# Every second product of the adaptive parameters on POOL and ACT instead of DVE

## The chip, the cores and the metric

The kernel runs on one core of a Trainium2 chip. The metric is the device time of one execution in microseconds (us). The engines named below are PE (matrix products), PEld (its weight loads), DVE (vector), ACT (scalar), POOL (GpSimd) and SP (the queue that issues most DMAs).

## The reference

Two blocks follow each other on 256 tokens of width 1024. The first has two layers, each with a mixer (latent attention and a chunked mLSTM) and a convolutional FFN; the second is one layer with three token mixers and a hierarchical mixture of 32 experts. Each layer takes its shifts, scales and gates from a conditioning vector c, by one product of a vector with a 1024 x 6144 matrix. That product is what the change touches:

```python
c_act = jax.nn.silu(c)
for l in range(DEPTH):
    mod = (c_act @ ada_w[l] + ada_b[l])[:, None, :]
    sh1, sc1, g1, sh2, sc2, g2 = jnp.split(mod, 6, axis=-1)
    h = _rmsnorm(x, norm_mix_w[l]) * (1 + sc1) + sh1
    x = x + g1 * _mixer(h, ...)
    h = _rmsnorm(x, norm_ffn_w[l]) * (1 + sc2) + sh2
    x = x + g2 * _conv_ffn(h, ...)
```

The second block has the same form, and uses its matrix w_ada twice: all six parts for the tokens (c_2), and the first two parts for a context of 256 tokens (c_ctx_2).

## The kernel before

**Weights.** Nearly all matrix products are made of float32 split in two: a weight block of 128x1024 is loaded, ACT casts it to a rounded form (`hi`, line 451), DVE takes the residual (`lo`, line 453), and PE makes three products for each pair of operands (lines 474 to 476). `load` (line 442) brings 128x2048 at a time into a tile `raw` of which there are three; all such loads, weights and the matrix of the adaptive parameters alike, are issued on SP in program order, each when its tile is free. `hi` and `lo` have three tiles each.

**Adaptive parameters.** `ada` (line 524) makes the product with c. Its matrix is stored transposed, so an output lies on a partition: one load gives two blocks `w` of 128 outputs x 1024 inputs. For each block one DVE operation (line 533) multiplies it with c (a tile `cb`, the same on all partitions, which holds twice the SiLU of c), by 0.5, and sums along the row into one column of `mod`. The operation writes its product back into `raw`; the profile shows it with a short read of the accumulator after it. A part is a 1024-wide slice of the six: four loads, eight columns, and then one addition of the bias (line 536).

**Order.** `ada` is a generator: it yields after each load. In the context pass at the start its first two parts are made in the foreground, since the first projections need them (`context`, with four `raw` tiles of its own). The first two parts of layer 0 then run in the background of the context pass, and ADA_PARTS (line 36) spreads the other sixteen parts over mixer 0 (4 parts), FFN 0 (3), mixer 1 (5) and FFN 1 (4). `tick` steps the background generators at fixed rates at points in the program. Within an engine the order is fixed when the program is made; each engine works through its own in that order, and waits where an operand or a tile isn't ready.

**Stages in the trace.** Context pass to about 110 us, mixer 0 to 335, FFN 0 to 560, mixer 1 to 775, FFN 1 to 1015, the second block's mixers to about 1315, and the experts to the end. The FFN's only regular work on POOL is the residual of its hidden values (`split` at line 459, tile `hidl`). DVE's line 1033 adds a product in PSUM to `x`.

Of the kernel before, what the change touches and what calls it, by code (L numbers as in the profile page):

```python
# [15 lines left out]
AF = mybir.ActivationFunctionType  # L16
OP = mybir.AluOpType
# [334 lines left out]
class Net:  # L352
# [162 lines left out]
    def silu_row(self, c, eng=None):  # L515
# [5 lines left out]
        nc.vector.scalar_tensor_tensor(t, th, 1.0, t, OP.add, OP.mult)  # L521
        return t

    def ada(self, src, c, bias, mod, parts, pool=None):

        nc = self.nc
        for s in parts:
            for q in range(4 * s, 4 * s + 4):
                raw = self.load(src[q], pool, 3 if pool is None else CX_RAW)
                for r in range(2):  # L530
                    j = 2 * q + r
                    w = raw[:, r * 1024 : r * 1024 + 1024]
                    nc.vector.scalar_tensor_tensor(w, w, 0.5, c, OP.mult, OP.mult, accum_out=mod[:, j : j + 1])  # L533
                yield
            m = slice(8 * s, 8 * s + 8)
            nc.vector.tensor_tensor(mod[:, m], mod[:, m], bias[:, m], OP.add)
# [1632 lines left out]
```

## Time and profile before

| | |
|---|---|
| median of 3 runs | 1775.16 us (1772.66 to 1775.33) |
| the profiled execution | 1772.79 us, its span 1770.9 us |
| PE busy | 1579.1 us, 89% |
| DVE busy | 1128.0 us, 64% |
| ACT busy | 758.6 us, 43% |
| POOL busy | 77.9 us, 4% |
| mean granted clock of PE | 0.946 of full speed |

Busy times are sums over instructions of the one profiled execution; a busy PE is not PE at its peak, since its ends are modelled. The chain that ended last is followed back from the last instruction, at each step to what released it. An engine's idle time off that chain costs nothing.

### The profile page before, as it was taken

The numbers are of one execution on the slowest core, as the hardware profiler recorded it, in microseconds if no ns is written. First come the engines' busy times: TensorE is split into PE (matmuls) and PEld (weight loads), VectorE is DVE, ScalarE is ACT, GpSimd is POOL, SyncE is SP. The second block draws the span as 40 slices with busy tenths as digits, with TensorE's granted clock in tenths as the row PEclk, the third lists the DMA queues.
The fourth block names the chain that finished last, engine by engine and source line by source line (L and its number), as shares of the span: only waits on it lengthen the run. The fifth ranks groups of instructions, "written<-read, shape, count | busy, mean of one in ns | idle before, by whom it ended". The sixth has DMA issues, their size and how long they took to land.

```text
span 1770.9 us, 32054 instructions
## 1 busy us (share of the span) xinstructions
PE 1579.1 (89%) x13278; PEld 1269.7 (72%) x13278; DVE 1128.0 (64%) x2167; ACT 758.6 (43%) x1256; POOL 77.9 (4%) x81
## 2 busy tenths in 40 slices
PE   3989999999998999989999999999989877776766
PEld 2988999899998899979999999878874312221211
DVE  7979878798887898879989778766662111011011
ACT  3566545664455654556454576464431100000000
POOL 0000000020010000001010101000000000000000
PEclk7999999999999999999999999998989889888888
DMA  9745675556674478565667543123369999999998
GB/s 392 312 142 191 242 281 204 209 207 221 217 250 143 169 266 319 216 237 179 239 228 289 194 171 114 67 98 134 144 249 403 419 417 416 417 416 419 419 417 340
DMA packets 76808, 460.78 MB, mean 260 GB/s; under 512 B 8563, under 2 KB 11123, under 8 KB 28147
## 3 DMA queue, kind: packets, MB, share of 16 engines
q1 hardware_dynamic: 74352, 452.45, 67.0%
q10 hardware_dynamic: 2306, 6.24, 1.0%
q8 instruction: 106, 1.74, 0.4%
q14 instruction: 44, 0.35, 0.1%
HBM read 457.61 MB, written 1.05 MB: 259 GB/s over the span
## 4 chain that ended last, share of the span: by engine, by line
PE 63%; DMA 23%; DVE 8%; ACT 4%; issue 2%; POOL 0%; SPq 0%; DVEq 0%; ACTq 0%; POOLq 0%
DMA ew<-in_wgu 11%; PE d L474 10%; PE d L476 10%; PE d L475 10%; DMA ew<-in_wdown 8%; PE y L474 4%; PE y L476 3%; PE y L475 3%; PE a L1392 3%; DVE lo L453 2%; PE d L2052 2%; DVE raw L533 2%; PE a L1981 1%; PE a L628 1%; DMA raw<-in_ws 1%
## 5 line engine op out<-in xcount | busy, mean ns | idle before, releaser
L451 ACT CAST hi<-raw 128x1024 fp32r<-128x1024 f32 x309 | 322.4, 1048 | 303.2 <-PE d L475 186.2
L453 DVE TENSOR_TENSOR lo<-raw,hi 128x1024 fp32r<-128x1024 f32 x309 | 379.1, 1233 | 90.3 <-ACT hi L451 88.5
L474 PE MATMUL d<-hhi,hi 128*128 128x256 f32 x1320 | 387.9, 295 | 29.4 <-ACT hhi L591 23.7
L475 PE MATMUL d<-hlo,hi 128*128 128x256 f32 x1320 | 381.3, 289 | 3.2 <-DVE hlo L594 1.7
L476 PE MATMUL d<-hhi,lo 128*128 128x256 f32 x1320 | 380.2, 288 | 0.2 <-DVE lo L453 0.2
L474 PEld LDWEIGHTS d<-hhi,hi 128*128 128x128 f32 x1320 | 258.4, 196 | 38.3 <-ACT hhi L591 26.3
L475 PEld LDWEIGHTS d<-hlo,hi 128*128 128x128 f32 x1320 | 259.3, 196 | 6.6 <-DVE hlo L594 2.9
L476 PEld LDWEIGHTS d<-hhi,lo 128*128 128x128 f32 x1320 | 259.0, 196 | 1.4 <-DVE lo L453 0.4
L2052 PE MATMUL d<-ew,xe 128*32 128x512 f32 x984 | 165.3, 704 | 56.5 <-DMA ew<-in_wgu 56.0
L533 DVE SCALAR_TENSOR_TENSOR raw<-raw,cb 128x1024 f32<-128x1024 f32 x160 | 193.9, 1228 | 5.4 <-DMA raw<-in_ada 5.0
L2052 PEld LDWEIGHTS d<-ew,xe 128*32 128x32 f32 x984 | 26.1, 116 | 170.5 <-DMA ew<-in_wgu 145.7
L2057 DVE SCALAR_TENSOR_TENSOR moa<-moa,d 128x512 f32<-128x512 f32 x8 | 5.5, 687 | 178.4 <-ACT moa L2056 178.4
L474 PE MATMUL y<-hhi,hi 128*128 128x256 f32 x352 | 100.8, 286 | 4.6 <-ACT raw L685 3.9
L476 PE MATMUL y<-hhi,lo 128*128 128x256 f32 x352 | 100.0, 285 | 0.9 <-DVE lo L453 0.9
L475 PE MATMUL y<-hlo,hi 128*128 128x256 f32 x352 | 99.6, 283 | 0.0
L2070 PE MATMUL y<-ew,mht 128*32 128x512 f32 x472 | 74.4, 687 | 26.6 <-DMA ew<-in_wdown 22.4
L2088 DVE SCALAR_TENSOR_TENSOR x<-f,mod_l,x 128x256 f32<-128x256 f32 x32 | 14.0, 479 | 127.8 <-PE f L2084 127.8
L459 POOL TENSOR_TENSOR hidl<-fgel,hidh 128x256 fp32r<-128x256 f32 x44 | 54.2, 1233 | 838.4 <-ACT hidh L458 817.3
L2056 ACT ACTIVATE moa<-d 128x512 f32<-128x512 f32 x8 | 4.8, 597 | 184.7 <-PE d L2052 184.7
L474 PEld LDWEIGHTS y<-hhi,hi 128*128 128x128 f32 x352 | 67.4, 192 | 6.1 <-ACT raw L685 4.7
L2070 PEld LDWEIGHTS y<-ew,mht 128*32 128x32 f32 x472 | 13.0, 117 | 78.3 <-DMA ew<-in_wdown 58.6
L476 PEld LDWEIGHTS y<-hhi,lo 128*128 128x128 f32 x352 | 67.4, 192 | 1.4 <-DVE lo L453 1.1
(676 smaller groups left out, 3193.7 us busy)
## 6 DMA issues: line engine op xcount, KB each, us to landing
raw<-in_ws SPq DMA_DIRECT2D x151, 1024.0 KB, 4.8
ew<-in_wgu SPq DMA_DIRECT2D x100, 1024.0 KB, 18.0
raw<-in_ada SPq DMA_DIRECT2D x80, 1024.0 KB, 4.9
ew<-in_wdown SPq DMA_DIRECT2D x46, 1024.0 KB, 19.7
ew<-in_wgu SPq DMA_DIRECT2D x46, 512.0 KB, 13.8
ew<-in_wdown SPq DMA_DIRECT2D x28, 512.0 KB, 12.5
two<-in_wgu SPq DMA_DIRECT2D x20, 256.0 KB, 8.4
two<-in_wdown SPq DMA_DIRECT2D x16, 256.0 KB, 8.1
```

The lines of the kernel that those rows point to most:

```text
L451: f.append(nc.scalar.copy(hi_, raw))
L453: f.append(nc.vector.tensor_tensor(lo_, raw, hi_.bitcast(F32), OP.subtract))
L459: (eng or self.nc.vector).tensor_tensor(lo, src, hi.bitcast(F32), OP.subtract)
L474: nc.tensor.matmul(out, whi, hhi, start=first and i == 0, stop=False, **s)
L475: nc.tensor.matmul(out, whi, hlo, start=False, stop=False, **s)
L476: nc.tensor.matmul(out, wlo, hhi, start=False, stop=last and i == n - 1, **s)
L533: nc.vector.scalar_tensor_tensor(w, w, 0.5, c, OP.mult, OP.mult, accum_out=mod[:, j : j + 1])
L628: self.nc.tensor.transpose(out, in_, self.C("ident")[:k, :k])
L1392: nc.tensor.matmul(ps[r, g * 64 : g * 64 + 64], l_(g, p, r), r_(g, p, r), start=True, stop=True, skip_group_check=True)
L1981: nc.tensor.matmul(ps[:, k * P : k * P + P], xn[:, i, d : d + P], of(i), start=i == 0, stop=i == 1, skip_group_check=True)
L2052: nc.tensor.matmul(ps[32 * e : 32 * e + 32, :], xe[:, k, 32 * e : 32 * e + 32], w[e], start=k == 0, stop=k == 7, skip_group_check=True)
L2070: nc.tensor.matmul(py[q][32 * e : 32 * e + 32, :], ht[:, f * P + 32 * e : f * P + 32 * e + 32], w[e], start=f == 0, stop=f == 3, skip_grou ...
```

## The change

A new function makes the product of one block. For the first block of each load POOL multiplies the block with c in place, and ACT then copies the result in place with the factor 0.5 and sums along the row; the second block stays as it was, one DVE operation. Loads, tiles, parts, rates and the addition of the bias are unchanged.

```diff
--- before.py
+++ after.py
@@ -521,6 +521,15 @@
         nc.vector.scalar_tensor_tensor(t, th, 1.0, t, OP.add, OP.mult)
         return t
 
+    def ada_block(self, w, c, out, shared):
+
+        nc = self.nc
+        if shared:
+            nc.gpsimd.tensor_tensor(w, w, c, OP.mult)
+            nc.scalar.activation(w, w, AF.Copy, scale=0.5, accum_out=out)
+        else:
+            nc.vector.scalar_tensor_tensor(w, w, 0.5, c, OP.mult, OP.mult, accum_out=out)
+
     def ada(self, src, c, bias, mod, parts, pool=None):
 
         nc = self.nc
@@ -528,9 +537,7 @@
             for q in range(4 * s, 4 * s + 4):
                 raw = self.load(src[q], pool, 3 if pool is None else CX_RAW)
                 for r in range(2):
-                    j = 2 * q + r
-                    w = raw[:, r * 1024 : r * 1024 + 1024]
-                    nc.vector.scalar_tensor_tensor(w, w, 0.5, c, OP.mult, OP.mult, accum_out=mod[:, j : j + 1])
+                    self.ada_block(raw[:, r * 1024 : r * 1024 + 1024], c, mod[:, 2 * q + r : 2 * q + r + 1], r == 0)
                 yield
             m = slice(8 * s, 8 * s + 8)
             nc.vector.tensor_tensor(mod[:, m], mod[:, m], bias[:, m], OP.add)
```

## Rows read from the trace of the kernel before

**Rows 1.** Page, parts 1 and 4: busy time, and the chain by engine.

```profile
PE 1579.1 (89%) x13278; PEld 1269.7 (72%) x13278; DVE 1128.0 (64%) x2167; ACT 758.6 (43%) x1256; POOL 77.9 (4%) x81
...
PE 63%; DMA 23%; DVE 8%; ACT 4%; issue 2%; POOL 0%; SPq 0%; DVEq 0%; ACTq 0%; POOLq 0%
```

**Rows 2.** Table of stretches: length, then busy PE, PEld, DVE, ACT, POOL.

```profile
41.00:110.00 69.00, 67.15 (x521) 64.28 (x521) 61.52 (x111) 42.74 (x56) 0.72 (x2) 0.95 0.71 273
110.00:335.00 225.00, 210.42 (x1675) 200.70 (x1674) 179.71 (x316) 129.33 (x213) 0.00 (x0) 0.99 0.61 220
...
560.00:775.00 215.00, 200.04 (x1556) 190.23 (x1555) 178.10 (x316) 119.54 (x202) 0.49 (x2) 0.97 0.65 237
```

**Rows 3.** Chain's shares by line: 0:50, 110:300, 335:560, 560:775.

```profile
by line: DMA raw<-in_ws 26.0%; DMA x<-in_xT 24.1%; DMA raw<-in_ada 17.5%; DVE raw L533 13.9%; DVE lo L453 4.7%; ACT hhi L591 2.7%; ACT hi L451 2.1%; issue 1.8%; ACT two L561 1.5%; SPq L442 1.4%; DVE two L590 1.0%; SPq L519 0.8%; ACTq L382 0
by line: PE d L474 14.1%; PE d L475 13.5%; PE d L476 13.2%; DVE lo L453 7.7%; DVE raw L533 5.7%; issue 4.5%; DVE cacc L765 3.2%; ACT hi L451 2.7%; DMA raw<-in_ws 2.5%; PE a L628 2.2%; PE a L847 1.8%; PE a L884 1.4%; ACT L548 1.4%; ACT L549 
by line: PE d L474 14.8%; PE d L475 14.3%; PE d L476 14.0%; PE y L474 13.1%; PE y L476 12.8%; PE y L475 12.5%; PE a L1392 5.8%; DVE lo L453 2.3%; issue 1.8%; DVE two L590 1.1%; PE a L1370 1.1%; DVE x L1033 1.0%; PE a L1479 0.7%; PE a L628 0
by line: PE d L474 15.1%; PE d L475 15.0%; PE d L476 14.9%; DVE lo L453 5.9%; DVE raw L533 4.7%; issue 3.1%; PE a L628 2.1%; PE a L847 2.0%; PE d L487 1.9%; ACT hi L451 1.9%; PE d L488 1.8%; PE d L489 1.8%; DVE cacc L765 1.7%; PE a L898 1.6
```

**Rows 4.** Groups of DVE (to 1010 us) and ACT (to 1000), by form.

```profile
L453 DVE TENSOR_TENSOR lo<-raw,hi 128x1024 fp32r<-128x1024 f32 x268 | 328.5, 1232 | 84.0 <-ACT hi L451 82.3
L533 DVE SCALAR_TENSOR_TENSOR raw<-raw,cb 128x1024 f32<-128x1024 f32 x160 | 193.9, 1228 | 5.4 <-DMA raw<-in_ada 5.0
...
L855 ACT ACTIVATION_READ_ACCUMULATOR esm<-a,mx 128x1 f32 x32 | 6.3, 197 | 0.0
...
L520 ACT ACTIVATE cbt<-cb 128x1024 f32<-128x1024 f32 x3 | 3.2, 1057 | 3.3 <-DMA cb<-in_c_c 3.3
```

**Rows 5.** POOL's two-input operations by source line: minimum/median/maximum in ns.

```profile
L459 POOL TENSOR_TENSOR hidl<-fgel,hidh x44: 726/1298/1825, 360.5 to 1008.3; 128x256 fp32r<-128x256 f32 x44
...
L1728 POOL TENSOR_TENSOR two<-two,kon x8: 994/999/1108, 1183.3 to 1283.4; 128x384 f32<-128x384 f32 x8
```

**Rows 6.** Timeline, three places: start us, duration us, engine, line, operation.

```profile
364.51 2.90 DVE L453 TENSOR_TENSOR lo<-raw,hi 128x1024 fp32r<-128x1024 f32 x2
...
364.71 1.61 POOL L459 TENSOR_TENSOR hidl<-fgel,hidh 128x256 fp32r<-128x256 f32 x1 [2.68 <-ACT hidh L458]
...
401.69 0.73 POOL L459 TENSOR_TENSOR hidl<-fgel,hidh 128x256 fp32r<-128x256 f32 x1 [5.79 <-ACT hidh L458]
401.78 0.88 DVE L1033 SCALAR_TENSOR_TENSOR x<-d,mod,x 128x256 f32<-128x256 f32 x2
...
860.86 1.82 POOL L459 TENSOR_TENSOR hidl<-fgel,hidh 128x256 fp32r<-128x256 f32 x1 [8.63 <-ACT hidh L458]
860.86 1.22 DVE L453 TENSOR_TENSOR lo<-raw,hi 128x1024 fp32r<-128x1024 f32 x1
```

**Rows 7.** Timeline of the start.

```profile
16.27 1.22 DVE L533 SCALAR_TENSOR_TENSOR raw<-raw,cb 128x1024 f32<-128x1024 f32 x1 [3.20 <-DMA raw<-in_ada]
...
27.29 2.36 DVE L453 TENSOR_TENSOR lo<-raw,hi 128x1024 fp32r<-128x1024 f32 x2 [1.19 <-ACT hi L451]
...
34.27 0.17 DVE L536 TENSOR_TENSOR mod_c<-mod_c,vec 128x8 f32<-128x8 f32 x1
...
35.82 0.80 PE L474 MATMUL d<-hhi,hi 128*128 128x256 f32 x2 [14.79 <-ACT hhi L591]
```

**Rows 8.** Table of stretches for line 453 alone (DVE).

```profile
110.00:335.00 225.00, 73.02 (x60) 0.99 0.61 220
```

**Rows 9.** Waits: engine, line, waited for: us in total, times, longest.

```profile
ACT hi L451 <- PE d L475: 186.2, 118, 7.2
...
ACT hi L451 <- DMA raw<-in_ws: 35.7, 27, 5.3
...
SPq L442 <- DVE raw L533: 192.9, 59, 9.1
```

**Rows 10.** Groups of ACT: loads of activation tables, the largest group.

```profile
L541 ACT ACT_TABLE_LOAD x25 | 32.1, 1283 | 0.4
```

## Prediction

> **What bounds the kernel now.** I read the page first: PE is busy 89% of the span, DVE 64%, ACT 43%, POOL 4%; the chain that ended last runs 63% on PE, 23% on DMA, 8% on DVE and 4% on ACT [rows 1]. So the change takes work from an engine with a small share of the chain and gives it to the idlest one. Where on the chain that DVE share lies decides, so the second view is the table of stretches [rows 2]. The reader is to see that PE is busy 67 of 69 us in 41:110, but only 210 of 225 us in the first mixer (110:335) and 200 of 215 us in the second (560:775). The expert stage from about 1315 us on holds none of the changed products; what happens before it moves it as a whole. Third, the chain by line in four stretches [rows 3]: the products (line 533) make 13.9% of 0:50 (7 us), 5.7% of 110:300 (10.8 us) and 4.7% of 560:775 (10.1 us); in FFN 0 (335:560) they are not among the lines named.
>
> **What it removes.** There are 160 products of 128x1024, two for each of 80 loads; 193.9 us of DVE, 1.21 us each [rows 4]. The change takes the first of each load: 80 products, 97 us of DVE. 8 lie in the first context pass (before 35 us), 8 in the second (to 110 us), 16 in mixer 0, 12 in FFN 0, 20 in mixer 1, 16 in FFN 1 (parts 0 and 1 twice, then ADA_PARTS, 4 loads a part). Only what lies on the chain can come back. In the mixers that is at most half of 20.9 us: -10.5 us. In the FFNs and the second context pass PE covers it: 0.
>
> **What POOL pays.** No POOL product of 128x1024 is in the trace. The nearest rows are its two-input operations: 726 ns at best with 256 columns, 999 ns median with 384 [rows 5]. That is 2.13 ns a column, so 999 + 640 x 2.13 = 2.36 us; with no fixed part at all it would be 2.66 us (999 x 1024/384). I take 2.36 us.
>
> **What DVE pays for POOL.** The rows show POOL and DVE holding each other up. At 364.71 POOL starts a product beside two residuals (lo); they take 2.90 us together, where an undisturbed pair takes 2.36 us [rows 6, 7]: the second one was held for 0.54 us. At 860.86 both start at once, the residual keeps its 1.22 us and POOL's 256-column product takes 1.82 us instead of 0.73 [rows 6]. At 401.69 POOL's product takes its 0.73 us beside two operations (line 1033) that read one operand from PSUM, and those take 0.88 us, undisturbed [rows 6]. So a DVE operation with two SBUF operands and a POOL product go one after the other, whoever comes first. The residuals alone, of this kind, are 328 us of DVE [rows 4], and the remaining products are of it too. A POOL product thus costs DVE between 0 (DVE idle, or at PSUM operations) and 2.36 us (the next operation has two SBUF operands), against the 1.21 us saved. DVE is busy about 80 to 90% in these stretches [rows 2]; I take 1.4 us.
>
> The Trainium skill (SBUF — State Buffer, § SBUF: two separate sides) states the same without a limit of size: the shared port pair is an exclusive lock, held for the whole instruction, and the loser fully blocks. The rows show it for holds up to about half a microsecond; no row here shows one of 2.4 us. By the rule the long hold blocks fully, as I count; were the two to share bandwidth instead, the sum below would lose its lock terms and come out near 1772 us.
>
> **What ACT pays.** The nearest rows are the activation of 128x1024, 1.06 us, and the accumulator read, 0.20 us [rows 4]: 1.25 us, 100 us in all. ACT is idle over 40% of both mixers [rows 2], so most of it finds room. But the sum waits for POOL, and behind it in ACT's order stand the casts (hi) that feed DVE's residuals and PE, and in the mixers the exponentials and copies of the heads.
>
> **The sum, part by part.**
> Start (0:41). The modulation sums must be complete before the first context projection: the bias is added at 34.27, PE starts at 35.82 after 14.79 us idle [rows 7]. The third load's products start at 16.27 after a wait of 3.20 us for its landing [rows 7]: DVE, with 2.4 us a load, keeps pace with the loads. With POOL a load takes 1.21 + 2.36 = 3.57 us, as the two products share one raw tile and one operand and exclude each other. Six loads from 16.27 on: 21.4 us, two residuals 2.36 us in between, the last sum 1.25 us: 41.3 instead of 34.3, +7.0 us. Below, if POOL runs beside DVE and ahead of the residuals, 0. I take +6, near the upper end, for the rows of the lock. PE is full in 41:110, so nothing of it is given back.
> Mixers, DVE. -10.5 us of chain as above; about nine of the 36 POOL products (10.5/1.21) stand where the removed ones were on the chain, each 0 to 2.36 us: 0 to +21, taken as 9 x 1.4 = +12.5. Net +2 (between -10.5 and +10.5).
> Mixers, ACT. 36 products, each 1.25 us and a wait for POOL of about a microsecond (the lock) ahead of others. Casts are 2.7% of the chain in 110:300 (5 us, five casts of 1.05 us) [rows 3], against 60 residuals, and so 60 casts, in that mixer [rows 8]: one in twelve. 36 x 2.25/12 = +7 us; 0 if always covered, 27 if one in three is not. I take +5.
> Loads. A raw tile is held until both products and the sum are done. Counted from its landing that was 2.4 us; it becomes 3.6 us (POOL first, then DVE beside ACT) to 4.8 us (DVE, POOL, ACT in a row). The loads are issued in order on SP, three tiles in turn, and SP waited 59 times, 192.9 us, for a product to free one [rows 9]; weights queue behind that. Some 59 issues are 1.2 to 2.4 us later. Casts waited for weights 27 times, 35.7 us [rows 9], and the 268 residuals to 1010 us [rows 4] are 134 loads: one load in five comes late. That a third of this reaches PE is an estimate: in 110:300 the chain has 4.8 us of weights' transfers [rows 3] of those 35.7 us. 59 x 1.8/5/3 = +7, between 0 and +21; I take +5, since SP often waits well ahead of the need.
> FFNs and second context pass. 36 products, PE-bound; casts wait for PE to free a buffer 118 times, 186.2 us [rows 9], so hi and lo run ahead. The residual on POOL (hidl) waits up to 2.36 us behind a product; it is used a group of blocks later. 0; without that cover up to +10.
> Sum: 6 + 2 + 5 + 5 = +18 us on the profiled execution's 1772.79 us: 1791 us. That execution is 2.4 us under the median of the runs shown (1775.16) and within their spread, so I leave it there.
>
> **Rivals.**
> 1. DVE's relief wins: the POOL products fall where DVE is idle or at PSUM operations, so the lock costs little, and casts and loads stay covered. -10.5 us in the mixers, +2 at the start: 1764 us. For it: DVE is idle 45 of 225 us in mixer 0 [rows 2]; against: the idle time is not where DVE is on the chain. It decides for faster from the point where a POOL product holds DVE for less than about 0.5 us on the chain (9 x 0.5 of the 8.5 us) with the start at +2.
> 2. PE hides all behind the start: +2 to +5, 1776 us. For it: PE is busy 93% or more in each stretch of [rows 2].
> 3. ACT's order carries the delay through: each of the 64 products behind the contexts blocks ACT for 2.25 us, and one in three reaches PE: +48 on top of the start's 6, 1827 us. For it: in the heads' loops PE, ACT and DVE hand work on in turn; against: ACT's idle time.
> 4. The sum needs an activation table of its own: 1.28 us a load [rows 10], two for each product, 205 us of ACT, up to 1996 us with the sum above. The Trainium skill (ScalarE: Activation LUTs, § Table sets: the hidden batching unit) says that copy is in every set, by which this falls away; no row here shows this form.
>
> **How the numbers follow.** Forecast 0.58; rival 1 0.13; rival 2 0.14; rival 3 0.13; rival 4 0.02. About 0.2% (3.5 us) is what a measurement of this kernel can tell from no change. Rival 1 is faster, rival 2 the same, the rest slower: 0.13, 0.14, 0.73. The range goes from 1768, which takes in rival 2 and the near part of rival 1, to 1825, the upper bounds of the loads, the mixers' ACT term and the start together and nearly rival 3.
>
> **What would show it.** The table of stretches: the first PE work at 41 us instead of 36; mixers longer by 3 to 10 us each; DVE busy time little changed, as stretched residuals replace the products. POOL's products at 2.4 to 3.6 us, 80 of them, some 200 us of POOL. Residuals with a maximum near 3.6 us. ACT waiting for POOL some 80 times, about 1 us each. SP waiting on ACT's sum instead of DVE's product. The prediction is wrong if residuals beside a POOL product keep 1.2 us, if the start doesn't move, or if the mixers are shorter.

## The result: 87 us slower, five times the forecast's loss

The kernel after takes 1861.46 us (median; 1857.29 to 1866.36) against 1774.13 us of the kernel before: a ratio of 1.0494, 95% interval 1.0464 to 1.0523. That is +87 us where +18 us was forecast; 1861 us lies 36 us above the upper end of the range. The profiled execution took 1863.36 us, its span 1861.3 us.

Lines of the kernel after stand seven lower from the change on: the product on POOL is line 528, its sum on ACT 529, the product left to DVE 531, the residual is still line 453. First the page of the kernel after, its busy times (part 1) and its groups (part 5: busy us, mean ns | idle just before, releaser), which answer to [rows 1, 4]:

```profile
PE 1603.7 (86%) x13278; PEld 1290.6 (69%) x13278; DVE 1167.8 (63%) x2014; ACT 832.6 (45%) x1407; POOL 300.1 (16%) x161
...
L453 DVE TENSOR_TENSOR lo<-raw,hi 128x1024 fp32r<-128x1024 f32 x309 | 431.6, 1402 | 105.6 <-ACT hi L451 102.4
...
L528 POOL TENSOR_TENSOR raw<-raw,cb 128x1024 f32<-128x1024 f32 x80 | 224.3, 2808 | 581.7 <-DMA raw<-in_ada 398.8
...
L531 DVE SCALAR_TENSOR_TENSOR raw<-raw,cb 128x1024 f32<-128x1024 f32 x80 | 127.5, 1596 | 29.7 <-DMA raw<-in_ada 29.6
...
L529 ACT ACTIVATE raw<-raw 128x1024 f32<-128x1024 f32 x80 | 84.7, 1059 | 132.0 <-POOL raw L528 131.8
```

The first number to read is DVE's. Eighty products of 1.21 us left it, 97 us, so 1128.0 us [rows 1] should have become 1031; it became 1167.8. DVE spends 137 us more on what it kept, 1.7 us for each product on POOL. Residuals went from a mean of 1233 ns (1232 for those of [rows 4]) to 1402, the products still on DVE from 1228 ns [rows 4] to 1596. PE's row is the second: the same 13278 matmuls are busy 25 us longer than in [rows 1].

Where the time came in is shown by cutting both traces at the same work: at the start of the sum of squares ahead of each stage (start with the first context pass, second pass with mixer 0, FFN 0, mixer 1, FFN 1, then what follows, without products). Tables of stretches, columns as in [rows 2] with PE's granted clock behind the bracket of POOL. Before:

```profile
0.00:49.00 49.00, 18.37 (x87) 16.48 (x88) 37.23 (x75) 17.60 (x25) 0.19 (x4) 0.79 0.98 394
49.00:319.00 270.00, 253.57 (x2017) 241.77 (x2017) 221.95 (x401) 158.31 (x252) 0.72 (x2) 0.99 0.62 227
319.00:554.00 235.00, 230.77 (x2258) 222.83 (x2257) 199.08 (x346) 130.43 (x202) 27.45 (x22) 0.99 0.60 212
554.00:776.00 222.00, 207.04 (x1614) 197.17 (x1613) 184.31 (x326) 124.00 (x208) 0.49 (x2) 0.97 0.65 234
776.00:1013.00 237.00, 231.05 (x2252) 222.82 (x2252) 206.28 (x374) 126.94 (x198) 26.80 (x22) 0.99 0.63 225
1013.00:1306.00 293.00, 286.10 (x2975) 246.86 (x2974) 211.17 (x468) 159.84 (x291) 21.89 (x28) 0.98 0.36 132
```

The same six stretches after:

```profile
0.00:62.00 62.00, 21.31 (x91) 18.70 (x92) 41.68 (x58) 28.81 (x45) 29.37 (x15) 0.78 0.87 338
62.00:351.00 289.00, 260.87 (x2016) 247.86 (x2015) 226.83 (x356) 175.66 (x292) 59.19 (x23) 0.96 0.56 208
351.00:599.00 248.00, 231.06 (x2251) 222.86 (x2250) 204.85 (x322) 141.19 (x225) 59.69 (x34) 0.99 0.55 201
599.00:849.00 250.00, 218.20 (x1623) 207.32 (x1622) 201.94 (x290) 143.14 (x245) 57.53 (x22) 0.93 0.56 208
849.00:1103.00 254.00, 235.37 (x2248) 225.75 (x2248) 213.13 (x342) 142.58 (x230) 72.07 (x38) 0.97 0.59 210
1103.00:1396.00 293.00, 286.05 (x2975) 246.80 (x2974) 211.47 (x468) 159.99 (x291) 21.84 (x28) 0.98 0.36 132
```

Column by column: the stages grew by 13, 19, 13, 28 and 17 us, and the last, which has no product on POOL, by 0. Every stage with products pays, the FFNs too. Over the first five rows the length grows by 90 us, PE's busy time by 26 (940.8 to 966.8 us) and its idle time by 64. Most of the 26 us go with the granted clock: it fell from 0.99 to 0.96 in the second stage (PE busy 7 us more), from 0.97 to 0.93 in mixer 1 (11 us) and from 0.99 to 0.97 in FFN 1 (4 us). The start's 3 us don't show in its clock (0.79 and 0.78).

Now what one product does. Places in the timeline after (start us, duration us, engine, line; in brackets idle before and releaser): the start, a head of mixer 1, FFN 0.

```profile
30.78 5.84 POOL L528 TENSOR_TENSOR raw<-raw,cb 128x1024 f32<-128x1024 f32 x2 [1.94 <-DMA raw<-in_ada]
31.08 6.63 DVE L453 TENSOR_TENSOR lo<-raw,hi 128x1024 fp32r<-128x1024 f32 x2
...
40.10 0.17 DVE L543 TENSOR_TENSOR mod_c<-mod_c,vec 128x8 f32<-128x8 f32 x1
41.65 0.80 PE L474 MATMUL d<-hhi,hi 128*128 128x256 f32 x2 [15.90 <-ACT hhi L598]
...
44.09 6.69 DVE L601 SCALAR_TENSOR_TENSOR hlo<-two,mod_c,hhi 128x256 fp32r<-128x256 f32 x6
44.25 5.06 POOL L528 TENSOR_TENSOR raw<-raw,cb 128x1024 f32<-128x1024 f32 x2 [7.62 <-DVE cb L521]
...
694.98 2.40 POOL L528 TENSOR_TENSOR raw<-raw,cb 128x1024 f32<-128x1024 f32 x1 [7.13 <-DVE qk L776]
695.23 2.19 DVE L859 TENSOR_SCALAR mx<-mx 128x2 f32<-128x2 f32 x1
697.51 0.37 ACT L862 ACTIVATE esm<-a,mx 128x128 f32<-128x128 f32 x1 [3.43 <-DVE mx L859]
...
408.87 2.40 POOL L528 TENSOR_TENSOR raw<-raw,cb 128x1024 f32<-128x1024 f32 x1 [3.74 <-DMA raw<-in_ada]
409.02 3.33 DVE L453 TENSOR_TENSOR lo<-raw,hi 128x1024 fp32r<-128x1024 f32 x1
```

Two residuals that took 2.36 us [rows 7] take 6.63 beside two POOL products. At 409.02 a residual that starts 0.15 us after a product ends with it plus its own 1.1 us. That is the rule in this trace: of 31 residuals that begin inside a product on POOL, 30 end 1.08 us after its end, whenever they began; the 16 that had begun before the product keep their length. At 695.23 the wait is longer than the work many times over: 2.19 us for two columns, and ACT, idle for 3.43 us by then, starts its exponential only behind it. POOL is no more than 16% busy, and yet a DVE operation that begins inside one of its products can be stopped until the product's end.

### The profile page after: what moved, and what is told of

It reads as the page before. It is cut to its first block, busy times and chain, and to the rows that moved or that the text cites. A ratio compares the mean times of both kernels' runs of the same rounds, so it can differ in the third digit from the quotient of the medians.

```text
span 1861.3 us, 32316 instructions
## 1 busy us (share of the span) xinstructions
PE 1603.7 (86%) x13278; PEld 1290.6 (69%) x13278; DVE 1167.8 (63%) x2014; ACT 832.6 (45%) x1407; POOL 300.1 (16%) x161
## 5 line engine op out<-in xcount | busy, mean ns | idle before, releaser
L453 DVE TENSOR_TENSOR lo<-raw,hi 128x1024 fp32r<-128x1024 f32 x309 | 431.6, 1402 | 105.6 <-ACT hi L451 102.4
L474 PE MATMUL d<-hhi,hi 128*128 128x256 f32 x1320 | 392.7, 298 | 28.8 <-ACT hhi L598 20.0
L475 PE MATMUL d<-hlo,hi 128*128 128x256 f32 x1320 | 386.3, 293 | 7.8 <-DVE hlo L601 4.8
L476 PE MATMUL d<-hhi,lo 128*128 128x256 f32 x1320 | 385.3, 292 | 2.0 <-DVE lo L453 1.9
L528 POOL TENSOR_TENSOR raw<-raw,cb 128x1024 f32<-128x1024 f32 x80 | 224.3, 2808 | 581.7 <-DMA raw<-in_ada 398.8
L474 PEld LDWEIGHTS d<-hhi,hi 128*128 128x128 f32 x1320 | 262.9, 200 | 38.7 <-ACT hhi L598 22.3
L475 PEld LDWEIGHTS d<-hlo,hi 128*128 128x128 f32 x1320 | 264.3, 200 | 11.2 <-DVE hlo L601 6.1
L476 PEld LDWEIGHTS d<-hhi,lo 128*128 128x128 f32 x1320 | 263.7, 200 | 3.9 <-DVE lo L453 2.9
L531 DVE SCALAR_TENSOR_TENSOR raw<-raw,cb 128x1024 f32<-128x1024 f32 x80 | 127.5, 1596 | 29.7 <-DMA raw<-in_ada 29.6
L529 ACT ACTIVATE raw<-raw 128x1024 f32<-128x1024 f32 x80 | 84.7, 1059 | 132.0 <-POOL raw L528 131.8
```

What stands on the lines that cost most here:

```text
L453: f.append(nc.vector.tensor_tensor(lo_, raw, hi_.bitcast(F32), OP.subtract))
L474: nc.tensor.matmul(out, whi, hhi, start=first and i == 0, stop=False, **s)
L475: nc.tensor.matmul(out, whi, hlo, start=False, stop=False, **s)
L476: nc.tensor.matmul(out, wlo, hhi, start=False, stop=last and i == n - 1, **s)
L528: nc.gpsimd.tensor_tensor(w, w, c, OP.mult)
L529: nc.scalar.activation(w, w, AF.Copy, scale=0.5, accum_out=out)
```

## The experiments

All comparisons are with the kernel before on the same chip. Edits are shown against the kernel after unless said otherwise.

### Is it ACT? The sum on ACT, the product on DVE (dve_act)

```diff
-            nc.gpsimd.tensor_tensor(w, w, c, OP.mult)
+            nc.vector.tensor_tensor(w, w, c, OP.mult)
```

> The first block's product by DVE (one operation with two SBUF operands), the sum by ACT as in the change; no POOL. DVE has the load of before, ACT the 100 us more of the change, and ACT waits for DVE instead of POOL. Theory lock: +0 to +15 us against before. Theory wait (ACT's place in order matters, whoever makes the product): +30 us or more.

1773.57 us against 1772.95; 1.0003 (0.9978 to 1.0029). Its page:

```profile
PE 1573.8 (89%) x13278; PEld 1265.7 (72%) x13278; DVE 1128.1 (64%) x2090; ACT 841.6 (48%) x1413; POOL 78.7 (4%) x81
```

ACT has all the sums (83 us more of busy time), in the same order of emission, and the time is that of before. The sums by themselves, with 33.7 us of ACT's waiting for DVE's product, cost nothing that can be measured; the 131.8 us of waiting for POOL in the change are another matter.

### What is the relief worth? The product cut to 64 columns (tiny)

```diff
+            w, c = w[:, :64], c[:, :64]
             nc.gpsimd.tensor_tensor(w, w, c, OP.mult)
```

> POOL's product and ACT's sum over 64 columns instead of 1024 (the rest of these blocks is left out). All instructions stay, their lengths go, and DVE keeps its relief of 97 us. Theories lock and wait: -15 to +5 us against before; the lower end is what the relief is worth by itself. If the new order of the work on PE, DVE and ACT, which the planner made around the new operations, were the cause: +30 us or more.

1762.84 us against 1772.95; 0.9946 (0.9921 to 0.9970): -10 us. DVE is busy 1050.3 us, 78 us less than before. So taking the products off DVE is worth 10 us when POOL's part is nearly nothing. All the new instructions are there and the planner has ordered the engines anew around them, so a new order as such doesn't bring a loss.

### The sum emitted one step later (late)

```diff
-            nc.scalar.activation(w, w, AF.Copy, scale=0.5, accum_out=out)
+            self.late.append((w, out))
...
             for q in range(4 * s, 4 * s + 4):
+                self.flush()
```

> POOL's product as in the change, but ACT's sum of a load stands one background step later in the program (at the last load of a part, at its end), so that POOL is mostly done when ACT comes to it. Theory wait: ACT's 132 us of waiting for POOL fall below 50 and the time to +30 to +45 us against before. Theory lock: the residuals stay at 1.40 us mean and +70 us or more stay; tiles held longer could add some.

1870.98 us, 1.0545 (1.0514 to 1.0576), a little slower than the change. It was to take away ACT's wait and did not: ACT's waits (us, times, longest) name the product as before.

```profile
ACT raw L528 <- POOL raw L535: 136.6, 55, 8.5
```

The planner places each instruction by its own table of costs, so emitting the sum later didn't put it later. The run says nothing on what the wait is worth.

### POOL busy without the product: memsets (memset, memset_64)

```diff
-            nc.gpsimd.tensor_tensor(w, w, c, OP.mult)
+            for t in (w, w, w[:, :512]):
+                nc.gpsimd.memset(t, 0.0)
```

> POOL writes zeros over the block (two and a half memsets, about 2.4 us, no operand read from SBUF) instead of multiplying it; ACT sums the zeros, so the first block of each load is left out of the result. POOL is busy as long and ACT waits for it as before. Theory lock (POOL's products hold DVE's operations with two SBUF operands): the residuals go back to 1.23 us and most of the 87 us goes: +10 to +35 us against the kernel before. Theory wait (ACT stands at its place in order until POOL is done, and PE starves behind it): +65 us or more stay.

5720 us. The zeros change the modulation and with it the routing: experts get more than 32 tokens, and the loop for the overflow runs. Only what lies ahead can be read: the last residual starts at 1283.0 us, before at 1294.1, 11 us earlier. The second try keeps 64 real columns, which leaves the routing where it doesn't overflow:

```diff
-            nc.gpsimd.tensor_tensor(w, w, c, OP.mult)
+            nc.gpsimd.tensor_tensor(w[:, :64], w[:, :64], c[:, :64], OP.mult)
+            for t in (w[:, 64:], w[:, 64:], w[:, 64:512]):
+                nc.gpsimd.memset(t, 0.0)
```

> POOL multiplies 64 columns and writes zeros over the other 960 two and a half times (about 2.5 us in all, nearly nothing read from SBUF), ACT sums the block: the same parameters come out as with 64 columns alone, so nothing of the later routing differs from that run. The blocks' other 960 columns are left out. Theory lock: -5 to -15 us against before, as with 64 columns alone. Theory wait (ACT waiting for a POOL that is busy 2.4 us): +30 us or more.

1786.08 us against 1775.19; 1.0067 (1.0046 to 1.0088). Page, busy times, and the residuals' group:

```profile
PE 1577.1 (88%) x13278; PEld 1270.4 (71%) x13278; DVE 1050.0 (59%) x2017; ACT 836.1 (47%) x1406; POOL 309.2 (17%) x401
...
L453 DVE TENSOR_TENSOR lo<-raw,hi 128x1024 fp32r<-128x1024 f32 x309 | 377.0, 1226 | 137.3 <-ACT hi L451 135.3
```

POOL is busy as long as after the change (309 against 300 us) and DVE is as free as in the kernel with 64 columns: residuals at 1226 ns. A POOL that is busy, but doesn't read, holds nobody. What is left, +11 us against that kernel's -10, is to about one half a longer start: its first residual comes at 37.1 us instead of 27.3, and its first stage takes 61 us where the other's takes 49. It isn't ACT's waiting for POOL, which is shorter here (61.1 us in 48 waits) than with 64 columns alone (70.7 us in 47); the other half stays open. The start has its own reason. Rows of POOL by source, and its timeline:

```profile
L528 POOLq MODIFY_POOL_CONFIG  x2: 11/11/11, 8.8 to 8.8; - x2
```

```profile
7.84 0.90 POOL L530 MEMSET raw<- 128x960 f32 x1 [7.41 <-DMA raw<-in_ada]
19.93 0.31 POOL L528 TENSOR_TENSOR raw<-raw,cb 128x64 f32<-128x64 f32 x1 [11.19 <-DVE raw L533]
```

A memset runs at 7.84 us; then POOL is configured at 8.8, and its first product starts 11 us later. The row names a DVE product as releaser, but that belongs to another load's raw tile by its time (it began at 18.63, when the first load's own had ended at 9.1), so I take the gap for the configuration's; it isn't proved.

### The product without any relief or sum: POOL does it in addition (extra)

Against the kernel before:

```diff
                     nc.vector.scalar_tensor_tensor(w, w, 0.5, c, OP.mult, OP.mult, accum_out=mod[:, j : j + 1])
+                    if r == 0:
+                        nc.gpsimd.tensor_tensor(w, w, c, OP.mult)
```

> The kernel before, both products on DVE, and after the first one POOL multiplies the used block once more; nobody reads that and ACT has nothing new. Theory stalls (DVE's being held is enough by itself to reach PE): 80 x 1.3 us of stalls without any relief, +80 us or more against before. Theory chained waits (the held POOL product makes ACT wait, and ACT the casts): +10 to +40 us, since nobody waits for POOL here.

1883.86 us against 1775.19; 1.0623 (1.0576 to 1.0670): +109 us.

```profile
PE 1616.8 (86%) x13278; PEld 1298.7 (69%) x13278; DVE 1264.8 (67%) x2167; ACT 759.4 (40%) x1256; POOL 312.4 (17%) x161
```

DVE has the same 2167 instructions as before [rows 1] and is busy 136.8 us longer, the 137 us of the change once more. ACT has nothing of POOL's to wait for. The presence of the product alone costs more than the change.

### The product without the sum (nosum), and the same with one operand (oneop_nosum)

```diff
-            nc.gpsimd.tensor_tensor(w, w, c, OP.mult)
-            nc.scalar.activation(w, w, AF.Copy, scale=0.5, accum_out=out)
+            nc.vector.scalar_tensor_tensor(w[:, :64], w[:, :64], 0.5, c[:, :64], OP.mult, OP.mult, accum_out=out)
+            nc.gpsimd.tensor_tensor(w[:, 64:], w[:, 64:], c[:, 64:], OP.mult)
```

> The first block of each load: DVE multiplies and sums 64 columns, POOL multiplies the other 960 (2.2 us or more), which nobody reads; ACT has no sum. The 960 columns are left out of the result. DVE has its relief and is held by POOL as in the change, but ACT waits for nothing of it. Theory stalls (DVE's being held reaches PE by itself): +55 to +95 us against before. Theory chained waits (most of the change's loss goes over ACT's waiting for the held POOL product): -10 to +30 us. In between both have their part.

The second differs from it in the last line only:

```diff
-            nc.gpsimd.tensor_tensor(w[:, 64:], w[:, 64:], c[:, 64:], OP.mult)
+            nc.gpsimd.tensor_scalar(w[:, 64:], w[:, 64:], 0.0, None, OP.mult)
```

> As the run without the sum, but POOL's operation on the other 960 columns is a multiplication by a constant: one operand from SBUF, 2.6 us as measured, so longer than the product, and the tile is held longer. The 960 columns are left out of the result. Theory lock of two-operand work: DVE isn't held (residuals 1.23 to 1.25 us) and the +78 us of that run go: -15 to +5 us against before. Theory tile (the raw tile that comes free later, and the loads behind it): +50 us or more stay.

Two operands: 1851.88 us against 1773.81; 1.0439 (1.0411 to 1.0468), +78 us. One operand: 1778.86 us against 1773.35; 1.0038 (1.0014 to 1.0063), +5.5 us. Busy times (page), POOL's operation by source (ns, minimum/median/maximum) and the residuals' group; two operands first:

```profile
PE 1593.0 (86%) x13278; PEld 1285.6 (70%) x13278; DVE 1190.9 (65%) x2175; ACT 755.9 (41%) x1250; POOL 278.5 (15%) x161
...
L529 POOL TENSOR_TENSOR raw<-raw,cb x80: 2204/2294/3947, 11.0 to 1039.5; 128x960 f32<-128x960 f32 x80
...
L453 DVE TENSOR_TENSOR lo<-raw,hi 128x1024 fp32r<-128x1024 f32 x309 | 402.8, 1308 | 83.7 <-ACT hi L451 82.1
```

One operand:

```profile
PE 1575.0 (89%) x13278; PEld 1269.7 (71%) x13278; DVE 1095.5 (62%) x2175; ACT 756.6 (43%) x1250; POOL 306.4 (17%) x161
...
L529 POOL TENSOR_SCALAR raw<-raw x80: 2599/2627/4272, 12.1 to 972.8; 128x960 f32<-128x960 f32 x80
...
L453 DVE TENSOR_TENSOR lo<-raw,hi 128x1024 fp32r<-128x1024 f32 x309 | 384.0, 1247 | 108.2 <-ACT hi L451 105.6
```

This pair decides. Instruction counts of DVE and ACT are equal, the raw tile is tied up even longer by the one-operand form (2627 against 2294 ns), POOL is busier, and no engine uses POOL's result. POOL's operation differs, one operand instead of two, and with it how long DVE is held. By an estimate DVE would be busy 1055 us here without any hold (1128.0 less the 97 us of products, plus 80 short products of 0.225 us with accumulator reads of 0.08): two operands hold it for 136 us, one for 40. The 95 us between them come with 73 us of time.

One operand holds DVE too, but not to the end of POOL's operation. Two places in the timeline of that kernel:

```profile
192.19 2.61 POOL L529 TENSOR_SCALAR raw<-raw 128x960 f32<-128x960 f32 x1 [8.43 <-DVE est L987]
193.31 1.22 DVE L453 TENSOR_TENSOR lo<-raw,hi 128x1024 fp32r<-128x1024 f32 x1
...
491.59 2.61 POOL L529 TENSOR_SCALAR raw<-raw 128x960 f32<-128x960 f32 x1 [7.58 <-DMA raw<-in_ada]
491.63 2.03 DVE L453 TENSOR_TENSOR lo<-raw,hi 128x1024 fp32r<-128x1024 f32 x1
```

The residual at 491.63 begins 0.04 us after POOL's operation and takes 0.8 us more than alone; the one at 193.31 begins 1.1 us after it and isn't held, though POOL is still at work when it ends. Of 45 residuals that begin inside such an operation 11 are held, all of them begun in its first microsecond, and all end 0.55 us before POOL does; the 31 begun after the first microsecond take 1.19 to 1.23 us. With two operands 16 of 18 are held, until the product's end.

The late release of the tile is no cause, and the sum's wait isn't needed for the loss: without ACT's part 78 of the 87 us remain.

### A slower POOL with ACT waiting for it (pieces, oneop)

```diff
-            nc.gpsimd.tensor_tensor(w, w, c, OP.mult)
+            for i in range(0, 1024, 256):
+                nc.gpsimd.tensor_tensor(w[:, i : i + 256], w[:, i : i + 256], c[:, i : i + 256], OP.mult)
```

> The change with POOL's product in four pieces of 256 columns, 0.73 us each instead of one of 2.4 us. If the length of one hold is what costs (DVE can go between the pieces): residuals near 1.3 us mean, +20 to +55 us against before. If the sum of the holds costs, or POOL goes from piece to piece without letting DVE in: +85 us or more; ACT's wait grows in both.

1915.40 us, 1.0817 (1.0761 to 1.0874). Groups of its page:

```profile
L529 POOL TENSOR_TENSOR raw<-raw,cb 128x256 f32<-128x256 f32 x320 | 353.8, 1138 | 511.1 <-DMA raw<-in_ada 367.5
...
L530 ACT ACTIVATE raw<-raw 128x1024 f32<-128x1024 f32 x80 | 84.6, 1058 | 245.2 <-POOL raw L529 245.2
```

DVE gets in between the pieces: it is busy 1105.9 us instead of 1167.8. But a piece takes 1138 ns instead of 726 [rows 5], four take 4.4 us, and ACT waits 245 us instead of 132. The hold has moved from DVE to POOL and from there to ACT.

```diff
-            nc.gpsimd.tensor_tensor(w, w, c, OP.mult)
+            nc.gpsimd.tensor_tensor(w[:, :64], w[:, :64], c[:, :64], OP.mult)
+            for _ in range(2):
+                nc.gpsimd.tensor_scalar(w[:, 64:], w[:, 64:], 0.0, None, OP.mult)
```

> As the run before, but POOL multiplies the other 960 columns by zero twice, with one operand read from SBUF each time, about 2.5 us in all. These columns are left out of the result. If any POOL operation that reads SBUF holds DVE: residuals at 1.35 us mean or more and +50 us or more against before. If only two operands do: residuals at 1.23 us and -5 to -15 us.

2000.82 us, 1.1259 (1.1208 to 1.1310). The edit was sized wrongly, since one of these operations takes 2.6 us and not 1.2: a load costs POOL 6.4 us (two of 2844 ns mean, one of 709). What it shows is the price of waiting: DVE is held for some 39 us (busy 1089.5 us against 1050.3 with 64 columns alone), and ACT stands long.

```profile
ACT raw L531 <- POOL raw L530: 298.6, 68, 11.6
```

In order behind the waiting sum stand ACT's casts and exponentials, so this second mechanism exists and is costly from some length on. In the change itself ACT waits 131.8 us, and the kernel without the sum puts what that is worth at about 87 - 78 = 9 us. It is no exact bound, as that kernel has 80 short products more on DVE.

### Two mends that failed (warm, hidl_dve)

POOL's first product starts at 12.99 us although its data are there at 8.4. A one-column operation at the program's start was to take whatever happens once:

```diff
         nc.vector.memset(self.one, 1.0)
+        self.warm = self.cp.tile([P, 1], F32, name="warm")
+        nc.gpsimd.tensor_tensor(self.warm, self.one, self.eps6, OP.mult)
```

> The change with one POOL product of a single column at the very start, so that POOL's first use is out of the way when the first block lands. In the change POOL starts its first product 4.6 us after the block has landed. If that is POOL's first use: the products of the start end 3 to 5 us earlier and the time falls by 2 to 5 us against the change (+83 to +86 us against before). If the late start comes from elsewhere: no change (+88 us).

1866.70 us, 1.0500 (1.0467 to 1.0534): no gain. The one column itself starts no earlier (timeline), since the configuration stands at 0.8 us in the change already and some 12 us pass behind it (the row names DVE's `gw` as releaser, which is no operand of this operation):

```profile
13.13 0.18 POOL L372 TENSOR_TENSOR warm<-one,eps 128x1 f32<-128x1 f32 x1 [12.70 <-DVE gw L622]
```

If a product on POOL is so dear, the 44 residuals of the FFNs that POOL has had all along could be worth moving to DVE, in the kernel before:

```diff
-self.split(hh, hl, g, nc.gpsimd)
+self.split(hh, hl, g)
```

> The kernel before, with the 44 residuals of the FFN's hidden values on DVE (0.42 us each, 18 us) instead of POOL (0.73 us without DVE in the way). If POOL's holding of DVE costs at this size as well: 44 x 0.3 us or so of held residuals go, and the time falls by 2 to 8 us. If DVE's 18 us weigh more: 2 to 10 us longer.

1777.47 us against 1773.81; 1.0019 (0.9999 to 1.0040): not faster. Holds of 0.73 us by 256 columns, 44 of them, are not worth undoing. No version tried beats the kernel before with its whole computation.

## Why the prediction was wrong

**The step that failed** is "FFNs and second context pass. 36 products, PE-bound; ... hi and lo run ahead ... 0", together with the count of "about nine of the 36 POOL products" in the mixers. Both came from one thought: that a hold costs only where a removed product stood on the chain. The products removed had been placed by the planner into DVE's spare time, so their removal is worth little, as forecast; but a hold doesn't fall on the product that was there. It falls on whatever DVE has next, a residual, a hlo or a head's maximum, and for these PE, directly or through ACT, does wait: in FFN 0 its own waits for residuals and hlo are 5.5 us (hlo 2.2, residuals 1.8 and 1.5), where the same view of before lists none. How the rest of the loss reaches PE wasn't followed wait by wait. Holds count wherever they fall, not at nine of the products alone: +13 and +17 us in the FFNs, +19 (with the second context pass) and +28 in the mixers, against 0 and some +7 forecast. DVE idle 45 of 225 us, or "casts wait for PE", was taken as cover for a stop of 2.4 us that comes at any moment; it is an average, and the cover at that moment is what counts.

**The price of one hold was nearly right, its multiplier wrong.** Forecast were 1.4 us of DVE for each product; 137/80 = 1.7 us was measured, and again 136.8 us by the extra product. What this is in time was measured in two ways. The product without a sum, with the relief taken off, gives 78 + 10 = 88 us, 1.1 us for each product; the product in addition gives 109 us, 1.4 us for each. Multiplied by 80, the forecast's own 1.4 us less its relief of 10.5 would have come to +102, near the measured +87; multiplied by nine it came to +2. The two measurements don't close: 88 less 10 and plus 9 for ACT's part is 87 by construction, but 109 less 10 is 99. One reading is that DVE has less room for a stop where it keeps all its products; no run separates that.

**PE's clock was missing from the sum.** Bubbles of PE cost more than their length. Timeline of mixer 1, tables of 10 us (length, busy PE and so on, granted clock), the loop of the heads, before and then after:

```profile
660.00:670.00 10.00, 10.00 (x83) 9.55 (x82) 8.63 (x16) 5.10 (x11) 0.00 (x0) 1.00 0.91 318
```

```profile
710.00:720.00 10.00, 7.83 (x64) 7.49 (x64) 7.54 (x12) 5.39 (x11) 3.27 (x1) 1.00 0.56 211
720.00:730.00 10.00, 9.76 (x68) 9.55 (x69) 6.91 (x9) 4.45 (x10) 6.01 (x2) 0.83 0.63 220
```

Before, PE is busy 10 of 10 us at full clock. After, a stretch in which it is busy 7.83 us is followed by one with a granted clock of 0.83, part of it at 1.2 instead of 2.4 GHz: 68 matmuls keep PE busy for 9.76 us, where 83 (not the very same ones) took 10.00. Summed over the five stages PE's busy time grew by 26 us for the same work. The granted clock of the whole span fell from 0.946 to 0.934, which by itself makes 1599 us of 1579.1, an estimate of 20 us: about a quarter of the loss is the clock's.

**The start: right to its first matmul, short behind it.** PE was to start at 41 us instead of 36; it starts at 41.65, +5.8 us against a forecast +6. But the stage ends 13 us late. At 44.09 six hlo operations take 6.69 us beside two more products, where four took 1.66 us before (at 37.47), so 2.5 us for six; 4 us are lost there, and ACT's last two hhi of the context come at 53.35 and 53.76. "PE is full in 41:110, so nothing of it is given back" was true; that more would be lost in the same way I didn't count.

**The lock's rule.** The rows of before showed holds of up to half a microsecond; those of after show two of about 2 us (409.02 and 695.23), and 30 residuals that wait for a product's end. The Trainium skill (SBUF — State Buffer, § SBUF: two separate sides) states that the loser blocks for the whole instruction, and for POOL's products the trace agrees. It also states that a DVE operation with two SBUF inputs is blocked by a GpSimd operation that reads SBUF. With one operand the trace agrees for the first microsecond only of 2.6 us; where page and measurement differ the measurement decides. The short hold leaves residuals at 1247 ns (+5.5 us in all), the long one makes them 1308 ns (+78 us): it is the form with two operands on POOL that makes the hold dear.

**Small terms.** POOL's product: 2.36 us forecast, 2328 ns at least, 2574 in the median, 2808 in the mean with holds. ACT's sum: 1.25 us forecast, 1.06 + 0.19 measured. Loads: +5 forecast, and wrong in sign by this row: casts waited for weights 35.7 us before [rows 9] and 11.3 us after, probably because everything behind the loads became later than they. ACT waits for POOL 53 times, 2.5 us each, where 80 times about 1 us were forecast. SP waits for DVE's products 65 times, 265.9 us, and for ACT's sums 28 times, 87.1 us; forecast were the sums in place of the products. The mixers' ACT term of +5 is within the 9 us that the sum adds. Residuals reach 3427 ns (3.6 forecast). DVE's busy time "little changed" came out at +40 us; that was the first sign.

**Relief: right in size, in part by luck.** -10.5 us were forecast, in the mixers alone; -10 were measured with 64 columns. The table of that kernel, for the second stage, mixer 1 and the stage without products:

```profile
49.20:309.50 260.30, 250.19 (x2019) 239.32 (x2018) 200.89 (x361) 159.80 (x290) 15.14 (x24) 1.00 0.65 239
...
543.10:758.90 215.80, 203.23 (x1614) 194.69 (x1613) 166.08 (x291) 126.07 (x243) 13.68 (x22) 0.98 0.66 241
...
993.70:1291.80 298.10, 291.39 (x2973) 252.50 (x2971) 209.97 (x467) 159.57 (x291) 22.29 (x28) 0.95 0.36 130
```

Against before (270, 222 and 293 us) the first two are 10 and 6 us shorter, but the last, in which nothing was changed, is 5 us longer; the FFNs give 3 us together. So the products were worth some 19 us where they stood, and a part was lost again elsewhere.

**The rivals.** The relief (1764 us) and PE's cover (1776 us) fall: the first exists, as the kernel with 64 columns at 1762.84 shows, and would need a POOL that holds nobody. ACT's order (1827 us) is nearest in time but is not the cause: some 9 us of the 87 are its, though with a slower POOL it costs far more. A table load for the sum (1996 us) doesn't exist: ACT's copies took 1.06 us, and no load stands on their line.

**What stays open.** The planner makes a new order of all engines for each kernel, so some five microseconds between two variants can be its doing, as in the stage without products above. The 9 us of the sum and the 88 of the hold are taken as additive, which the kernels with a slower POOL (ACT's waits of 245 and 299 us, +140 and +226 us) don't support as a rule at every size.

## What to carry to other kernels

A two-operand elementwise operation on POOL is paid by DVE: count every one of them as a stop of DVE, here of two thirds of its length on average (1.7 of 2.57 us), not only those on the chain, and ask what DVE has next in line at that moment. Work that was placed in an engine's spare time is worth little when taken away (97 us off DVE gave 10), while unplanned stops of the same engine are paid for the most part (88 to 109 us of 137), PE's clock included. Before moving work, run it in addition, or cut it to a few columns: the two runs show cost and relief separately, if not to the last ten microseconds.

## Of the hardware, not expected

- POOL's one-operand multiplication of 128x960 takes 2.6 us, longer than the two-operand product of the same size (2.2 to 2.3 us), and holds residuals on DVE in its first microsecond only. A memset of 128x960 takes 0.90 us and leaves residuals at 1226 ns, as if alone.
- A DVE operation on 128x2 elements with one tensor operand was held for 2 us by a POOL product (695.23), so being held isn't confined to large operations or to those with two operands.
- POOL's first elementwise operation starts some 10 to 13 us after POOL is configured, whatever its size and although the data land by 8.4 us: configured at 0.8 us, it starts at 12.99 in the change (1024 columns), at 13.13 with the single column and at 11.03 in the product without a sum (960 columns); configured at 8.8, at 19.93 (64 columns, behind a memset; there a wait for DVE isn't excluded). Memsets run before it. In the kernel before POOL's first such operation comes at 360.49 us, so nothing shows there.
